# A streaming encoder layer on one core: the samples' key tiles in a pool of their own, the rope tables in a small pool, a norm factor among the constants

## The chip, the cores and the metric

The kernel runs on one core of a Trainium2 chip. The metric is device time in microseconds; of several runs of a kernel the median counts. The engines are TensorE (PE; its weight loads are PEld), VectorE (DVE), ScalarE (ACT), GpSimd (POOL) and SyncE (SP), which issues most of the transfers. ACT issues some transfers too.

## What is computed

One layer for 1024 tokens of a prompt and for 8 batches of 16 new tokens ("samples") with 1024 cached positions each. Cut to what matters here:

```python
u, g_pool, c_q, c_kv, k_r, g_mla = split(rms_norm(x, norm_g) @ w_in)
pool_out = multiscale_pool(...) * silu(g_pool)
q = (rms_norm(c_q, q_norm_g) @ w_uq).reshape(B, T, 8, 128 + 64)
q_nope = rms_norm(q[..., :128], q_nope_g)
q_rope = apply_rope(rms_norm(q[..., 128:], q_rope_g), cos, sin)
ckv_all = concat([ckv_hist, rms_norm(c_kv, kv_norm_g)])    # the samples' history is the cache
krope_all = concat([krope_hist, apply_rope(rms_norm(k_r, k_rope_g), cos, sin)])
kv = (ckv_all @ w_ukv).reshape(B, S, 8, 128 + 128)
k_nope, v = rms_norm(kv[..., :128], k_nope_g), kv[..., 128:]
attn = chunk_causal_attention(q_nope, q_rope, k_nope, krope_all, v)
h = x + concat([pool_out, attn * silu(g_mla)]) @ w_out
y = h + sigmoid(rms_norm(h, ple_norm_g) @ w_ple_gate + b_ple_gate) * (p @ w_ple)
```

All values are float32.

## The kernel before

Every product of float32 numbers is formed from high and low parts in three matmuls (`mm3`, lines 77 to 79); `split` (lines 68 and 69) makes the parts, the high one mostly on ACT (`ch`, `wh`, `m3h`, `qhl`), the low one on DVE (`cl`, `wl`, `m3l`). The phases are: 1, the input projection; 2, normalised latents and the prompt's keys, values and queries, a tile of 128 tokens at a time; 4, attention of the samples over their cache, then of the prompt, a head at a time, with pieces of the output projection (`f`) in between; 5, the rest of the output projection, the gate and the embedding. The per-layer embedding's projection (class `Embed`) is cut into units that are laid between other products where TensorE would wait: six matmuls into the one bank `p`, a copy `ev` on DVE (line 500; two buffers), and a store `ple<-ev` from ACT's queue (line 501); the next unit's weights `wraw<-w_ple` are loaded from ACT's queue as well (line 492).

**Phase 2.** `latent` loads a tile's raw latents (`rawcq`, `rawckv`), scales them and splits them (`cqh`, `cql`). `keys` forms keys and values (bank `pb`), evicts the values to `vv` and stores them (line 614). `queries` multiplies with the weights `wq` (four groups of two loads `raw<-w_uq`, split to `wqh`, `wql`), takes inverse norms (`inv_norms`: squares at lines 583 and 585, sums at 586, mean at 587, Newton steps at lines 86 to 90), applies them (line 595), and turns the rope part with the tables `qc` and `qs` (lines 640 and 332 to 335). `keys_out`, `queries_out` and `rotary_out` transpose (bank `pt`), evict (lines 625, 654 and 666) and store kT, qT and qrT. `queries_out` multiplies with the column `gqk`, the product of two norm gains and the scale.

**The samples' attention** (`attend_samples`). `keys(b, f)` loads half a batch's cached latents (`raw<-cache_T`, 512 KB) and rope keys (`kraw<-cache_krT`, two loads of 128 KB) and splits them to `ch`, `cl` and `ks`; `scores` forms the keys (bank `k`) for their norms and the scores; `queries(b)` splits the mapped queries of a batch into `m3h`, `m3l` and `qhl`, of which `m3h` and `m3l` also hold the last head of w_k (lines 1104 and 1105). `weigh` is the softmax and its product, in banks `aux`.

**Memory and order.** On-chip memory is handed out in pools. Those on the left side form a stack: during phase 2 these are p2a (value weights wvh and wvl, raw loads, `gqk`), p2c (latents, wq, the rope tables), p2b (all else). After phase 2 the pool p4k of the samples takes their place, at the same addresses. A tile waits for the last readers of what lay at its place (`reuse_waits="tile"`). The order of instructions on each engine isn't written by hand: a scheduler goes through the program with a timeline of its own and takes each engine's next instruction. It takes a new pool only when the pools whose place it uses have been given up, so a pool's place decides when the first instructions that use its tiles can be ordered. Transfers go round eight lanes; an issue waits for the transfer before it on its lane.

Of the kernel before, what the change touches and what calls it, by code (L numbers as in the profile page):

```python
# [6 lines left out]
F32R = mybir.dt.float32r  # L7
# [5 lines left out]
DRAM = bass.MemoryType.DRAM  # L13
# [6 lines left out]
P = 128  # L20
KT = D // P
TB = 384
# [16 lines left out]
class K:  # L39
    """Shared handles: the context, constants and small helpers."""  # L40
# [6 lines left out]
    def later(self, gen):  # L47
        """Start a piece of work that TensorE's next blocks of products interleave with."""
        if next(gen, self) is not self:
            self.queue.append(gen)  # L50

    def tick(self):
        """Take each piece under way to its next stop."""
# [9 lines left out]
    def split(self, hi, lo, src, scale=None, eng=None):  # L63
        """src (times a per-partition scale) as hi + lo, each of float32r's width."""
# [9 lines left out]
    def mm3(self, out, sh, sl, mh, ml, start, stop):  # L74
        """out += (sh + sl)^T (mh + ml) without the product of the two low parts."""
# [5 lines left out]
    def rsqrt(self, pool, y, v, tag):  # L81
        """y = v ** -0.5 for v > 0, by Newton steps from an exponent-halving seed."""
# [10 lines left out]
    def spread(self, pool, ps, out, r):  # L93
        """out[:, j * P + q] = r[q, j] on every partition."""
# [9 lines left out]
def load_w(k, wp, src, chunks=range(KT // WKC), scales=None, bufs=5):  # L104
    """Row chunks of a column tile of a weight [128, KT, 128], as hi and lo tiles of WKC row tiles."""
# [17 lines left out]
def project(k, ps, w, xh, xl, kts=range(KT)):  # L123
    """psum[128, TB] = w^T x over the row tiles kts, of which x holds just these."""
# [6 lines left out]
def phase1(k, sc):  # L131
    """Input projection, gates, pooling mixer, rope key; low-rank latents and row factors to DRAM.

    Stops once where the next phase's first loads can start.
    """
    tc, nc, io = k.tc, k.nc, k.io
    es, left = ExitStack(), ExitStack()
    # the first block's input leaves before the others'
# [14 lines left out]
    # order of the column tiles: latents and rope key first, gates of B last  # L153
# [19 lines left out]
    # x^T times the norm's gain, split; the row factors of the first norm  # L173
    w0 = {}
    with tc.tile_pool(name="p1x", bufs=1, side="right", reuse_waits="tile") as xp:
        for t in range(NT):
            # the very first pieces are short
# [13 lines left out]
    def row_factor(xp, t, j):  # L191
        """Sums of squares of token tile j of block t; after the last one the block's row factors, in steps."""
# [14 lines left out]
    def latent_factor(lp, kind, t, acc):  # L207
        """The row factors of a block's latents, from the lanes' sums of squares."""
# [28 lines left out]
    # latents: raw projections and their row factors, normalised where they are read back  # L237
# [41 lines left out]
    # gates and the pooling mixer; a group's map follows one block behind its input  # L279
# [37 lines left out]
def rope_tables(k, pool, tcos, tsin, gain2, scale):  # L317
    """Cosine and signed sine tables of all positions times the gain of the element they meet."""
# [1062 lines left out]
```

## Time and profile before

| | |
|---|---|
| Runs | 2322.14, 2326.36, 2325.97 us; median 2325.97 |
| Span of the profiled execution, from its first to its last instruction | 2321.7 us |
| The profiled execution's own time, with what lies around the span | the profile gives none |
| Busy PE, DVE, ACT, POOL | 2263.2, 1153.4, 844.8, 382.3 us |
| Mean granted clock of TensorE | 0.990 |
| Moved by DMA | 271.05 MB |

"Busy" counts the time in which an engine's instructions run; matmuls are pipelined, so a busy PE isn't at its peak. The granted clock is the share of TensorE's full speed: in this profile it is 1.0 or 0.5 in any short stretch, and 0.990 over the span means that some stretches ran at 0.5. A row of waits reads: the engine and line that waited, for what, us in total, times, the longest. A row of the timeline reads: start, length, engine, line, operation, output from input, count, and in brackets the idle time before it and what ended it. SPq and ACTq are the queues in which SP and ACT issue transfers; the length there is that of the issue, not of the transfer.

### The profile page before, as it was taken

The page shows a single profiled execution, that of the slowest core. Times are in us where ns is not written, and L with a number is a line of the kernel's source. Part 1 is how long each engine was busy: PE and PEld are TensorE (multiplying, and loading weights), DVE is VectorE, ACT ScalarE, POOL GpSimd, SP SyncE. Part 2 cuts the span into 40 slices and gives each one's busy share as a digit, 9 for nine tenths or more (in the row PEclk, how much of TensorE's full clock was granted, in tenths as well). Part 3 has the DMA queues.
Part 4 walks back from the last instruction along what each step waited for, and adds up shares of the span by engine and source line. Part 5 has one row for each costly group of instructions (what it writes and reads, how often), then busy time and mean ns, then how long its engine had stood idle before and what let it go on. Part 6 is the DMA issues. An engine that isn't in the chain of part 4 may idle for free.

```text
span 2321.7 us, 35417 instructions
## 1 busy us (share of the span) xinstructions
PE 2263.2 (97%) x13198; PEld 2207.8 (95%) x13198; DVE 1153.4 (50%) x2636; ACT 844.8 (36%) x1967; POOL 382.3 (16%) x357
## 2 busy tenths in 40 slices
PE   8899999999999999989999799999999999999999
PEld 8899999999999989978898699999999999999998
DVE  6443111334312169868988865555553335344343
ACT  6421111111111166766665453434342234222222
POOL 0000000123300000014443342212002221111110
PEclk9999999999999999999999899999999999999999
DMA  7522212333312186573221663434263334223221
GB/s 279 171 98 69 74 65 82 70 88 92 81 61 75 47 244 185 152 221 104 83 68 54 217 204 126 152 128 150 88 190 100 110 106 130 85 86 101 85 86 63
DMA packets 219661, 271.05 MB, mean 117 GB/s; under 512 B 38112, under 2 KB 160480, under 8 KB 219488
## 3 DMA queue, kind: packets, MB, share of 16 engines
q1 hardware_dynamic: 199616, 242.43, 33.4%
q10 hardware_dynamic: 19872, 26.35, 3.4%
q8 instruction: 104, 1.70, 0.3%
q14 instruction: 69, 0.57, 0.1%
HBM read 196.10 MB, written 72.61 MB: 116 GB/s over the span
## 4 chain that ended last, share of the span: by engine, by line
PE 80%; DVE 8%; DMA 7%; issue 2%; ACT 1%; POOL 1%; SPq 0%; ACTq 0%; DVEq 0%; POOLq 0%
PE mm L79 18%; PE mm L77 18%; PE mm L78 18%; PE f L77 3%; PE f L79 3%; PE f L78 3%; DMA xnat<-xN 2%; PE k L78 2%; PE k L77 2%; PE k L79 2%; PE t L919 1%; PE pb L77 1%; PE pb L79 1%; PE o L79 1%; PE pb L78 1%
## 5 line engine op out<-in xcount | busy, mean ns | idle before, releaser
L77 PE MATMUL mm<-A0h,wh 128*128 128x384 f32 x736 | 250.3, 340 | 6.7 <-ACT A0h L71 5.9
L78 PE MATMUL mm<-A0h,wl 128*128 128x384 f32 x736 | 249.7, 339 | 1.0 <-DVE wl L69 1.0
L79 PE MATMUL mm<-A0l,wh 128*128 128x384 f32 x736 | 249.8, 339 | 0.0
L77 PE MATMUL mm<-A1h,wh 128*128 128x384 f32 x736 | 246.6, 335 | 0.2 <-ACT ev L263 0.2
L79 PE MATMUL mm<-A2l,wh 128*128 128x384 f32 x736 | 246.6, 335 | 0.0
L77 PE MATMUL mm<-A2h,wh 128*128 128x384 f32 x736 | 246.5, 335 | 0.0
L78 PE MATMUL mm<-A2h,wl 128*128 128x384 f32 x736 | 246.4, 335 | 0.0
L79 PE MATMUL mm<-A1l,wh 128*128 128x384 f32 x736 | 246.3, 335 | 0.1
L78 PE MATMUL mm<-A1h,wl 128*128 128x384 f32 x736 | 246.3, 335 | 0.0
L69 DVE TENSOR_TENSOR wl<-wraw,wh 128x512 fp32r<-128x512 f32 (+1 forms) x232 | 157.4, 679 | 153.4 <-ACT wh L68 147.7
L68 ACT ACTIVATE wh<-wraw 128x512 fp32r<-128x512 f32 (+1 forms) x236 | 137.4, 584 | 246.8 <-PE mm L79 193.6
L77 PEld LDWEIGHTS mm<-A0h,wh 128*128 128x128 f32 x736 | 139.3, 189 | 7.4 <-ACT A0h L71 5.9
L78 PEld LDWEIGHTS mm<-A0h,wl 128*128 128x128 f32 x736 | 139.2, 189 | 1.8 <-DVE wl L69 1.8
L79 PEld LDWEIGHTS mm<-A0l,wh 128*128 128x128 f32 x736 | 139.1, 189 | 0.2 <-DVE A0l L72 0.2
L79 PEld LDWEIGHTS mm<-A1l,wh 128*128 128x128 f32 x736 | 138.2, 188 | 1.0 <-DVE A1l L72 0.7
L77 PEld LDWEIGHTS mm<-A1h,wh 128*128 128x128 f32 x736 | 138.2, 188 | 0.8 <-ACT ev L263 0.5
L77 PEld LDWEIGHTS mm<-A2h,wh 128*128 128x128 f32 x736 | 138.2, 188 | 0.0
L79 PEld LDWEIGHTS mm<-A2l,wh 128*128 128x128 f32 x736 | 138.2, 188 | 0.0
L78 PEld LDWEIGHTS mm<-A2h,wl 128*128 128x128 f32 x736 | 138.2, 188 | 0.0
L78 PEld LDWEIGHTS mm<-A1h,wl 128*128 128x128 f32 x736 | 138.2, 188 | 0.0
L233 DVE TENSOR_TENSOR ev<-mm,R 128x384 f32<-128x384 f32 x48 | 26.8, 558 | 224.3 <-PE mm L79 224.3
L1239 DVE TENSOR_TENSOR ev<-mm,R 128x384 f32<-128x384 f32 x48 | 26.8, 557 | 174.1 <-PE mm L79 170.2
(437 smaller groups left out, 5511.6 us busy)
## 6 DMA issues: line engine op xcount, KB each, us to landing
wraw<-w_in SPq DMA_DIRECT2D x120, 256.0 KB, 3.1
wraw<-w_out SPq DMA_DIRECT2D x64, 256.0 KB, 3.6
wraw<-w_ple_gate SPq DMA_DIRECT2D x64, 256.0 KB, 3.3
xnat<-xN ACTq DMA_DIRECT2D x36, 256.0 KB, 3.5
ple<-ev ACTq DMA_DIRECT2D x48, 192.0 KB, 2.5
fev<-xT SPq DMA_DIRECT2D x48, 192.0 KB, 2.4
hp<-fev SPq DMA_DIRECT2D x48, 192.0 KB, 1.9
ev<-hp SPq DMA_DIRECT2D x48, 192.0 KB, 2.3
```

The source lines that it names most:

```text
L68: nc.scalar.activation(hi, src, AF.Copy)
L69: eng.tensor_tensor(lo, src, hi, ALU.subtract)
L77: mm(out, sh, mh, start=start, stop=False)
L78: mm(out, sl, mh, start=False, stop=False)
L79: self.last = mm(out, sh, ml, start=False, stop=stop)
L233: nc.vector.tensor_tensor(ev[:], ps[:, :TB], R[t][:], ALU.mult)
L919: nc.tensor.transpose(tp[:, x, :], e[:, (c + x) * P:(c + x + 1) * P], k.ident[:])
L1239: nc.vector.tensor_tensor(g[:], ps[:, :TB], R[t][:], ALU.mult)
```

## The change

The column `gqk` moves from p2a to the pool of the constants. The rope tables and their gain come to a new small pool p2d, between p2c and p2b. `raw`, `ch`, `cl`, `kraw` and `ks` of the samples come to a new pool p4c just beneath p4k; both are closed together. The addresses of all tiles stay within 32 bytes of what they were (those of the key tiles: from the place of wvh to that of the first wq groups); the instructions and their number are the same. Comments and docstrings are gone too, with their lines kept, so that line numbers rise by 1 from 741 on and by 2 from 997 on.

```diff
-    gqk = k.t(pl, [P, 1], "gqk")
+    gqk = k.t(k.cp, [P, 1], "gqk")
...
     pq = es.enter_context(tc.tile_pool(name="p2c", bufs=1, reuse_waits="tile"))
+    pr = es.enter_context(tc.tile_pool(name="p2d", bufs=1, reuse_waits="tile"))
     pw = es.enter_context(tc.tile_pool(name="p2b", bufs=1, reuse_waits="tile"))
...
-    qc = k.t(pq, [P, 9, DR], "qc")
-    qs = k.t(pq, [P, 9, DR], "qs")
-    rope_tables(k, pq, qc, qs, io["q_rope_g2"], SCALE)
+    qc = k.t(pr, [P, 9, DR], "qc")
+    qs = k.t(pr, [P, 9, DR], "qs")
+    rope_tables(k, pr, qc, qs, io["q_rope_g2"], SCALE)
...
-    kp = tc.tile_pool(name="p4k", bufs=1, reuse_waits="tile")
-    kb = kp.__enter__()
+    kp = ExitStack()
+    kc = kp.enter_context(tc.tile_pool(name="p4c", bufs=1, reuse_waits="tile"))
+    kb = kp.enter_context(tc.tile_pool(name="p4k", bufs=1, reuse_waits="tile"))
...
-        raw = k.t(kb, [P, 2, HK * P], "raw", bufs=2)
+        raw = k.t(kc, [P, 2, HK * P], "raw", bufs=2)
...
-        ch = k.t(kb, [P, 2, HK * P], "ch", F32R, bufs=3)
-        cl = k.t(kb, [P, 2, HK * P], "cl", F32R, bufs=3)
+        ch = k.t(kc, [P, 2, HK * P], "ch", F32R, bufs=3)
+        cl = k.t(kc, [P, 2, HK * P], "cl", F32R, bufs=3)
...
-        kraw = k.t(kb, [P, HK * P], "kraw", bufs=2)
+        kraw = k.t(kc, [P, HK * P], "kraw", bufs=2)
...
-        ks = k.t(kb, [P, HK * P], "ks", F32R, bufs=2)
+        ks = k.t(kc, [P, HK * P], "ks", F32R, bufs=2)
...
-    kp.__exit__(None, None, None)
+    kp.close()
```

What it moves shows in the order of each engine. The first place is the passage from phase 2 to the samples. SP before: the stores of kT, qrT and qT of the last tiles, then the cache's first loads (the number in a name is that of its buffer).

```order
L656 DMA qT_96<-T_9309 128x8x128
L626 DMA kT_94<-T_9323 128x8x128
L668 DMA qrT_97<-rT_9568 128x4x128
L656 DMA qT_96<-T_9576 128x8x128
L1016 DMA raw_9611<-cache_T 128x2x512
L1022 DMA kraw_9617<-cache_krT 64x512 x2
L1016 DMA raw_9771<-cache_T 128x2x512
L1022 DMA kraw_9777<-cache_krT 64x512 x2
```

SP now:

```order
L656 DMA qT_96<-T_9312 128x8x128
L1018 DMA raw_9618<-cache_T 128x2x512
L1024 DMA kraw_9624<-cache_krT 64x512 x2
L1018 DMA raw_9778<-cache_T 128x2x512
L1024 DMA kraw_9784<-cache_krT 64x512
L626 DMA kT_94<-T_9326 128x8x128
L668 DMA qrT_97<-rT_9571 128x4x128
L1024 DMA kraw_9784<-cache_krT 64x512
L1018 DMA raw_10046<-cache_T 128x2x512
L1024 DMA kraw_10052<-cache_krT 64x512 x2
```

The first loads of the cache have moved ahead of the last kT store and the last two qrT and qT stores; the last qT and qrT stores now stand behind eight further cache loads.

DVE at the same place, before: the mean, seed and Newton steps of query tile 7 (`v_1476`, `r_1477`, `rsa_9410`) with an `ev` and two `wl` of the embedding's units among them.

```order
L587 TENSOR_SCALAR v_1476_9394<-v_1476_9394 128x8
L666 COPY rT_9568<-pt_9569 128x512
L69 TENSOR_TENSOR wl_9907<-wraw_9904,wh_9906 128x256
L86 TENSOR_SCALAR r_1477_9395<-v_1476_9394 128x16
L88 TENSOR_TENSOR rsa_9410<-r_1477_9395 128x16
L500 COPY ev_9565<-p_9558 128x384
L89 SCALAR_TENSOR_TENSOR rsa_9410<-rsa_9410,v_1476_9394 128x16
L90 SCALAR_TENSOR_TENSOR r_1477_9395<-rsa_9410,r_1477_9395 128x16
L69 TENSOR_TENSOR wl_9923<-wraw_9920,wh_9922 128x256
L88 TENSOR_TENSOR rsa_9410<-r_1477_9395 128x16
```

DVE now, around the same steps:

```order
L500 COPY ev_9568<-p_9561 128x384
L587 TENSOR_SCALAR v_1476_9397<-v_1476_9397 128x8
L69 TENSOR_TENSOR cl_9621<-raw_9618,ch_9620 128x1024
L1027 TENSOR_TENSOR ks_9627<-kraw_9624,ks_9627 64x512
L86 TENSOR_SCALAR r_1477_9398<-v_1476_9397 128x16
L69 TENSOR_TENSOR wl_9930<-wraw_9927,wh_9929 128x256
L500 COPY ev_9924<-p_9917 128x384
L88 TENSOR_TENSOR rsa_9413<-r_1477_9398 128x16
L69 TENSOR_TENSOR wl_9946<-wraw_9943,wh_9945 128x256
```

`cl` and `ks` of the first key tile stand between the mean (line 587) and the seed (line 86); before, they stood behind the last rT copy. A second `ks` stands further on among the Newton steps.

Ahead of that on DVE now, right after the last key tile's norms:

```order
L595 TENSOR_TENSOR kn_9244<-kn_9244,r_1460_9280 128x512 x2
L1106 COPY m3h_1540_9631<-wkh_6960 128x2x128
L1107 COPY m3l_1541_9632<-wkl_6961 128x2x128
L1106 COPY m3h_1542_9633<-wkh_6960 128x2x128
L1107 COPY m3l_1543_9634<-wkl_6961 128x2x128
L500 COPY ev_9536<-p_9529 128x384
L69 TENSOR_TENSOR m3l_1541_9632<-qp_7121,m3h_1540_9631 128x2x128
L69 TENSOR_TENSOR qhl_9653<-qr_7122,qhl_9653 128x128
L69 TENSOR_TENSOR m3l_1543_9634<-qp_7121,m3h_1542_9633 128x2x128
L69 TENSOR_TENSOR qhl_10042<-qr_7122,qhl_10042 128x128
L587 TENSOR_SCALAR v_1476_9397<-v_1476_9397 128x8
```

The four copies and the low parts of `m3` and `qhl` stood behind line 335, the end of query tile 7's rotation, before. ACT's four high parts moved likewise: they now stand between the last eviction of query tile 7 (line 636) and its last two squares, and the first `ch` stands behind the second `wh` after them, ahead of a load `wraw<-w_ple` and a store `ple<-ev`.

The second place is the start of phase 2. SP before:

```order
L692 DMA mask_8572<-own 128x8
L235 DMA gm_12_71<-ev_7109 128x384
L547 DMA rawcq_7143<-cq_6_65 128x4x128
L547 DMA rawckv_1048_7195<-ckv_3_62 128x2x128
L321 DMA ropeg_7208<-q_rope_g 128x128
L322 DMA qc_7206<-rope_cos 128x576
L323 DMA qs_7207<-rope_sin 128x576
L548 DMA srow_7456<-s_cq_28_87 128x128
L538 DMA raw_7171<-w_uq 128x768
L555 DMA ckvT<-rawckv_1048_7195 256x1x128
L538 DMA raw_7175<-w_uq 128x768
L614 DMA v_95<-vv_7215 128x8x128
```

SP now:

```order
L321 DMA ropeg_7211<-q_rope_g 128x128
L322 DMA qc_7209<-rope_cos 128x576
L323 DMA qs_7210<-rope_sin 128x576
L235 DMA gm_12_71<-ev_7109 128x384
L692 DMA mask_8575<-own 128x8
L547 DMA rawcq_7146<-cq_6_65 128x4x128
L547 DMA rawckv_1048_7198<-ckv_3_62 128x2x128
L548 DMA srow_7459<-s_cq_28_87 128x128
L555 DMA ckvT<-rawckv_1048_7198 256x1x128
L614 DMA v_95<-vv_7218 128x8x128
L538 DMA raw_7174<-w_uq 128x768
L548 DMA srow_7564<-s_cq_28_87 128x128
```

The rope tables (`ropeg`, `qc`, `qs`) have moved ahead of the mask, a store of gates and the first raw latents; the first store of values has moved ahead of the two w_uq loads of group 1, which are `raw_7171` and `raw_7175` before and `raw_7174` and `raw_7178` now. They stood ahead of the store of values; now they begin right behind it. PE has more of the embedding's units ahead of the products that need these weights.

The third place is the start of the prompt's attention, where the first head's transposes and products `o` come earlier on PE, and the pieces `f` of the output projection later; DVE's `M0l`, `M1l` and `M2l` splits, which feed those, come later as well. Between the first key tiles and the last batch of the samples the order is nearly the same, as it is behind the prompt's first heads.

## The prediction

> **What bounds the kernel now.** I read the page's engine lines and its 40 slices first, to see what the time consists of.
>
> ```profile
> span 2321.7 us, 35417 instructions
> PE 2263.2 (97%) x13198; PEld 2207.8 (95%) x13198; DVE 1153.4 (50%) x2636; ACT 844.8 (36%) x1967; POOL 382.3 (16%) x357
> PE   8899999999999999989999799999999999999999
> ```
>
> TensorE (PE) is busy for 97% of the span, and the change neither adds nor removes a product. So only two things can move the time: PE's waits, and stretches at half clock. Outside the span's first slices, the slices below 9 stand near 840, 1015 and 1275 to 1330 us. I then asked for the stretches around them (columns: length; busy us and count of PE, PEld, DVE, ACT, POOL; granted clock; share of the DMA engines; GB/s).
>
> ```profile
> 835.00:850.00 15.00, 11.58 (x44) 9.85 (x43) 11.98 (x33) 8.95 (x26) 0.00 (x0) 0.73 1.01 303
> 842.05:852.29 10.24, 8.39 (x27) 7.88 (x26) 5.35 (x18) 4.74 (x10) 0.00 (x0) 0.50 1.02 323
> 850.00:1005.00 155.00, 154.44 (x895) 144.94 (x894) 129.45 (x410) 112.45 (x399) 2.28 (x8) 0.99 0.56 165
> 1005.00:1030.00 25.00, 17.91 (x90) 14.76 (x89) 17.85 (x48) 11.21 (x29) 0.73 (x1) 0.93 0.83 249
> 1022.96:1026.37 3.41, 1.62 (x8) 0.91 (x6) 1.26 (x3) 1.64 (x3) 0.00 (x0) 1.00 1.06 313
> 1026.37:1029.78 3.41, 2.96 (x8) 2.66 (x9) 1.98 (x4) 1.42 (x3) 0.51 (x1) 0.50 1.09 329
> 1090.00:1280.00 190.00, 179.39 (x1093) 168.61 (x1092) 169.84 (x332) 113.63 (x221) 86.22 (x52) 1.00 0.22 73
> 1280.00:1360.00 80.00, 66.18 (x342) 57.62 (x341) 66.68 (x132) 43.95 (x100) 39.76 (x33) 0.87 0.74 232
> ```
>
> Three places have something to lose or win: A, the start of phase 2 (835 to 850, 3.4 us of idle PE and a clock of 0.73); B, the passage to the samples (1005 to 1030, 7.1 us idle); D, the passage to the prompt's attention (1280 to 1360, 13.8 us idle, clock 0.87). Between them PE is full (155 us from 850) or, from 1090 to 1280 (C), held by chains whose order the change leaves alone; after 1360 the slices are all 9. The waits of PE at A and B, and one of D:
>
> ```profile
> PE pb L77 <- ACT vv L613: 1.8, 1, 1.8
> PE pb L78 <- DVE cql L69: 1.5, 1, 1.5
> ...
> PE k L77 <- ACT ch L68: 1.7, 1, 1.7
> PE k L78 <- DVE cl L69: 0.6, 1, 0.6
> ...
> PE s L77 <- ACT e L904: 1.4, 1, 1.4
> PE f L77 <- DVE fev L822: 0.9, 1, 0.9
> PE f L79 <- POOL M0l L69: 0.8, 1, 0.8
> ```
>
> **The change at B.** A pool is taken only when what lies beneath it is done with. The key tiles no longer lie over the rope tables or `gqk`, which query tile 7 reads last; so the first cache load, which SP (the engine that issues these transfers) sent at 1017.88 right behind the last qT store, now stands behind the store before that.
>
> ```profile
> 1003.61 0.36 SPq L656 DMA_DIRECT2D qT<-T  x1
> ...
> 1017.43 0.36 SPq L656 DMA_DIRECT2D qT<-T  x1
> 1017.88 0.67 SPq L1016 DMA_DIRECT2D raw<-cache_T  x1
> ```
>
> It can leave 0.45 us after that store, as now, at 1004.1, 13.8 us earlier; the rope keys' load still waits for the query weights' last reader. With the 6.5 us that such loads took (a row below) it lands at 1010.6. Gone with that are PE's waits for ch and cl, 1.7 + 0.6, and, if PE is then fuller, the stretch at half clock: 2.96 us of busy PE at 0.50 cost 1.5. Together −3.8.
>
> What is added is worked out on VectorE (DVE) and ScalarE (ACT), which feed the p units (a piece of the embedding's projection, six products, then a copy `ev`, then a store) that fill PE here, one after the other through one bank.
>
> ```profile
> 1007.24 0.56 DVE L500 COPY ev<-p 128x384 f32<-128x384 f32 x1 [4.13 <-PE p L79]
> 1010.70 0.17 DVE L86 TENSOR_SCALAR r<-v 128x16 int32<-128x16 int32 x1
> 1011.19 0.56 DVE L500 COPY ev<-p 128x384 f32<-128x384 f32 x1
> 1019.68 0.29 DVE L1104 CAST m3h<-wkh 128x256 fp32r<-128x256 f32 x1
> 1019.89 0.29 DVE L1105 CAST m3l<-wkl 128x256 fp32r<-128x256 f32 x1
> ...
> 1020.83 0.42 DVE L69 TENSOR_TENSOR m3l<-qp,m3h 128x256 fp32r<-128x256 f32 x1
> ...
> 1021.90 0.55 DVE L500 COPY ev<-p 128x384 f32<-128x384 f32 x1
> ...
> 1025.54 1.23 DVE L69 TENSOR_TENSOR cl<-raw,ch 128x1024 fp32r<-128x1024 f32 x1 [2.15 <-ACT ch L68]
> 1027.26 0.69 DVE L1025 TENSOR_TENSOR ks<-kraw,ks 64x512 fp32r<-64x512 f32 x1
> ...
> 1018.76 0.40 ACT L68 ACTIVATE m3h<-qp 128x256 fp32r<-128x256 f32 x1
> ...
> 1006.20:1008.00 1.80, 1.80 (x15) 1.76 (x14) 0.76 (x3) 1.77 (x7) 0.00 (x0) 1.00 0.08 21
> ...
> ple<-ev ACTq DMA_DIRECT2D x5, 192.0 KB, 2.0
> ...
> raw<-cache_T SPq DMA_DIRECT2D x3, 512.0 KB, 6.5
> ...
> ple<-ev ACTq DMA_DIRECT2D x4, 192.0 KB, 5.0
> ```
>
> On DVE, cl and two ks come into the middle of query 7's normalisation: 1.23 + 2 × 0.69 = 2.6. Out of it go the four m3 copies, 0.2 from start to start, so 0.8, which now fall into the idle 4.13, and the four m3l and qhl splits (1020.83 to 1021.90, 1.1), which move in front. Net +0.7. ACT's four splits of the same tiles now stand ahead of query 7's squares, but two p units lie between those and the step that needs them (L86, 1010.70), so I cost that at nothing; without this cover it is at most 4 × 0.40 = 1.6.
>
> The dearer item is in the rows of `ple<-ev`, the store of an ev: median 2.0 us to landing from 1006 to 1017.3, 5.0 from there to 1032, with cache loads under way. ev has two buffers, so an ev waits for the store of two units before. Two units took 1011.19 − 1007.24 = 4.0; with 5.0 of store and 0.56 of copy it is 5.6, so +1.6 for each two units that run beside cache loads. The first six loads are 1.5 MB (2 × 512 and 4 × 128 KB), 4.9 us at the 313 GB/s of the row from 1022.96; more follow when ch is split. That is one to two pairs out of four, +1.6 to +3.2; I take 2.2, nearer the low end, because the DMA engines are at a share of 0.08 just before 1008. B: −3.8 + 0.7 + 2.2 = −0.9. Ends: −3.8 if all of it hides, and, with two pairs, ACT's 1.6 and the half clock kept, −2.3 + 0.7 + 3.2 + 1.6 = +3.2.
>
> The Trainium skill (TensorE: Matmul & The Clock Gate, "HAM oscillation — how this bites in real kernels") says that PE falls to half clock after idle gaps over about 3.4 us. The rows differ: the half-clock stretch from 1026.37 follows one with PE busy 1.62 of 3.41 us, and no wait at B is over 1.7. By that rule the 1.5 of clock would not hang on these waits, and the whole sum would be −0.9 in place of −2.4; by the rows it goes when the stretch before is more than half busy.
>
> **The change at A.** The rope tables' loads move ahead of the first latents', and the first v store ahead of the w_uq loads of group 1.
>
> ```profile
> 828.63 0.33 SPq L235 DMA_DIRECT2D gm<-ev  x1
> 831.32 0.53 SPq L547 DMA_DIRECT2D rawcq<-cq  x1
> ...
> 836.71 0.58 ACT L613 ACTIVATE vv<-pb 128x512 f32<-128x512 f32 x1
> ...
> 839.43 5.96 DMA v<-vv
> 845.47 0.61 ACT vv L613
> ```
>
> The last two rows are of the chain of waits: the v store took 5.96, vv's buffer waited for it, and PE for vv, 1.8. vv was complete at 837.3 (836.71 + 0.58), so the store can leave about 1 us earlier, at 838.4, and without two loads of 384 KB before it (2.4 us at 323 GB/s): landing 842 to 844.4 instead of 845.39, so the wait of 1.8 shrinks by 1 to 1.8; I take 1.4. The half-clock stretch (8.39 busy at 0.50, 4.2 lost) spans three equal parts of 3.41; a shorter wait may spare none or one of them (1.4), and I take 0.4. rawcq goes behind 640 KB of tables (2 × 288 and 64 KB), 2.0 us at 323 GB/s; but SP stood still for 2.3 us before it (828.96 to 831.32), and three issues of 0.3 to 0.5 fit in there: +0.3. The two w_uq loads go 1.6 us later (512 KB); the order puts p units in front of the products that need them, so nothing, and 1.6 if that cover is gone. A: −1.4 − 0.4 + 0.3 = −1.5. Ends: −7.5 (both waits, 3.3, and all 4.2), and +3.6 (2.0 + 1.6).
>
> **At D** pieces of the output projection (f) come later among the first head's scores, and transposes and o products earlier. The three waits quoted are 3.1; f being later favours M0l and fev, while softmax chains with fewer f products beside them speak against it. I take 0, with −3.1 and +3.1 as ends. C: 0, same order.
>
> **Sum**: −0.9 − 1.5 + 0 = −2.4 against the profiled span of 2321.7, so 2319.3. The profile gives no time around the span; the three runs stand 0.4 to 4.7 above it. Against their median, 2325.97, I forecast 2323.6.
>
> **Rivals.**
> 1. Slower, at B. ch stands in ACT's queue ahead of two p units' loads and stores, and cl in DVE's ahead of L86. ACT gets to ch between the second and the third ev of before, about 1010 to 1011 (an estimate from the rows at 1007.24 and 1011.19); if the cache load lands later than that (with 6.5 us it comes at 1010.6), everything behind waits one for one, and all four pairs of units run beside loads, 4 × 1.6 = 6.4, and the half clock stays: −2.3 + 0.7 + 6.4 = +4.8. It decides from 1 us of lateness on. With A at 0: 2330.8. Against it: the share of 0.08 just before. The Trainium skill (DMA: Bandwidth & Descriptors, "Issuing engines are not separate DMA queues") has transfers of all queues interleave on the same 16 engines, so that ACT's stores would pay for SP's loads; the store rows at B agree, 2.0 against 5.0.
> 2. Faster, beyond what runs can miss: A's half clock goes with its waits (−6 of the −7.5) and B stays at −0.9: 2325.97 − 6.9 = 2319.1. For it: 842.05 follows right on the two waits. Against: the first wait (cql) has no reason to go.
> 3. Nothing follows: the loads come earlier and PE meets the same total of waits, since the p units run through one bank at DVE's pace: 2326.
> 4. D loses its 3.1, and A 1.6 by the w_uq loads, while B stays: −0.9 + 3.1 + 1.6 = +3.8, so 2329.8; 0.9 more, by f products that M0l keeps waiting, and it counts as slower.
>
> **Numbers.** Three runs of one kernel spread over 4.2 us, so 0.2% (4.65 us) is about what can be told from no change. My case and rival 3, between −4.6 and +4.6: 0.34 + 0.18 = 0.52. Rival 2, with kindred gains at D: 0.28. Rival 1: 0.13; rival 4: 0.07. Faster 0.28, same 0.52, slower 0.20. The range leaves out a tenth at each side: down to 2316 (A −7.5 with D at −2.5), up to 2331.5 (rival 1 with a little more).
>
> **What would show it.** Right: first raw<-cache_T issued before 1006; no wait of k for ch or cl; the v store issued ahead of w_uq group 1 and the wait for vv under 1 us; idle PE from 1005 to 1030 between 5 and 8 us. Wrong: ple stores over 5 us from 1008 on and p waiting 2 us and more for ev; cql later than 842; over 15 us of idle PE or more than 10 us of lost clock from 1280 to 1360; a changed clock where no order changed.

## The result and the profile after

The changed kernel takes 2340.20 us (median of 4 runs, 2337.62 to 2342.86) where the kernel before took 2326.16 beside it (4 runs, 2322.14 to 2329.96): a ratio of 1.0061, with a 95% interval of 1.0046 to 1.0075. It is slower, by 14.0 us; 2323.6 was forecast, and the range ended at 2331.5.

The head of the profile after, with the busy times and PE's slices:

```profile
span 2335.8 us, 35429 instructions
PE 2270.1 (97%) x13198; PEld 2212.1 (95%) x13198; DVE 1160.7 (50%) x2636; ACT 844.2 (36%) x1967; POOL 382.4 (16%) x357
PE   8899999999999989989999799999999999999999
```

The execution's own time is 2337.62, so 1.8 us lie around the span. The products are the same 13198, but PE is busy 6.9 us longer; the 12 more instructions are waits for semaphores. To find where the span's 14.1 us came in I took, from each trace, the starts of the first product of phase 2 (keys and values), of the samples' first product k and of the first score s of the prompt's attention, and the ends of phase 2's last product and of the last score. These cut the span into six stages (us). Where the expectations below speak of phase 5 at 607 or 612 us, they count from the last score to the last product; the column "output" goes on to the span's end, 5.4 to 5.7 us later.

| Kernel | phase 1 | phase 2 (has A) | passage (B) | samples (C) | prompt's attention (has D) | output | span |
|---|---|---|---|---|---|---|---|
| before | 826.9 | 179.2 | 19.4 | 300.7 | 383.0 | 612.4 | 2321.7 |
| after | 823.3 | 187.0 | 23.2 | 298.4 | 386.1 | 617.8 | 2335.8 |
| after − before | −3.6 | +7.8 | +3.8 | −2.3 | +3.1 | +5.4 | +14.1 |

So the stages of A, B and D each got longer, where −1.5, −0.9 and 0 were forecast. The forecast for B reaches further than the passage, though: its window ran to 1032, and before the passage ends at 1025.56, so that the stretch at half clock (1026.37 to 1029.78) and the wait of k for cl lie in the samples' stage there. Passage and samples together got 1.5 us longer. And two stages moved in which no engine's order differs (but for the place of `gqk`'s own instruction), phase 1 and the output.

**A, the start of phase 2.** The same stretch of 46.7 us of before and of after (columns as in the prediction's stretches); phase 2 begins at its start in after, and 3.6 us into it before:

```profile
823.30:870.00 46.70, 43.06 (x209) 39.10 (x208) 31.23 (x78) 31.41 (x97) 0.00 (x0) 0.89 0.81 245
```

```profile
823.30:870.00 46.70, 38.38 (x183) 32.56 (x182) 31.32 (x80) 29.22 (x91) 0.00 (x0) 0.96 0.81 248
```

Counted over 46.7 us from each kernel's own first product of phase 2, it is 210 products before and 182 after. The clock is better than before, 0.96 against 0.89, yet PE did 28 products fewer. The chain of waits of after at this place says what came late, and the table of PE's waits from 820 to 870 who paid:

```profile
825.88 6.25 DMA qc<-rope_cos
832.13 0.02 issue
832.15 3.96 DMA rawcq<-cq
836.11 0.02 issue
836.14 0.42 DVE rawcq L550 x2
```

```profile
PE p L78 <- DVE wl L69: 2.5, 2, 1.3
PE p L79 <- DVE l L69: 2.0, 1, 2.0
PE p L77 <- ACT h L68: 1.1, 1, 1.1
PE p L77 <- DVE ev L500: 1.0, 2, 0.7
PE p L77 <- DVE r L90: 0.7, 1, 0.7
```

The wait for vv is gone, as forecast. But SP sent rawcq only when the cosine table had landed, 6.25 us after the table's own issue. Before, SP had stood ahead of rawcq too; the table of its waits has this row for rawcq's line:

```profile
SPq L547 <- DMA raw<-w_uq: 2.3, 1, 2.3
```

In both kernels rawcq's issue waits for the transfer that went before it on its lane. Before, that is a load of w_uq; in the new order it is the cosine table, and the mask's load, one issue ahead, waits 3.5 us for the rope gain's in the same way. The first query product starts 14.8 us after the first product of phase 2 (11.5 before), and the embedding's p units, which the order now has stand in for it, are not fed in time. A smaller part of the 7.8 comes later in phase 2: PE waits 1.6 us for an ev up to 918.6, and a stretch at half clock follows (919.7 to 923.1) that before doesn't have.

**B, the passage.** PE's waits of after from 1000 to 1040, and the half-clock stretch in it (7.62 us busy at 0.50 in 10.2 us, and a second one of 3.4 from 1032.3; before, one of 3.4):

```profile
PE p L77 <- DVE ev L500: 3.0, 1, 3.0
PE pt L665 <- DVE qr L335: 2.1, 1, 2.1
PE p L77 <- DVE v L587: 1.1, 1, 1.1
PE p L77 <- DVE rsa L89: 0.7, 1, 0.7
```

```profile
1018.70:1028.90 10.20, 7.62 (x25) 6.71 (x26) 8.80 (x19) 4.43 (x8) 5.04 (x2) 0.50 0.96 307
```

k waits for ch and cl no more, and the first cache load left at 1007.75, 0.45 us behind the qT store at 1007.30, as forecast. Instead PE waits four times on DVE, in query tile 7's chain. What held DVE shows in its rows and POOL's:

```profile
1019.08 2.35 POOL L69 TENSOR_TENSOR cl<-raw,ch 128x1024 fp32r<-128x1024 f32 x1 [109.97 <-DMA qrT<-rT]
1026.20 2.69 POOL L69 TENSOR_TENSOR cl<-raw,ch 128x1024 fp32r<-128x1024 f32 x1 [4.77 <-DMA wraw<-w_ple]
```

```profile
1016.07 1.22 DVE L69 TENSOR_TENSOR cl<-raw,ch 128x1024 fp32r<-128x1024 f32 x1
1017.32 0.69 DVE L1027 TENSOR_TENSOR ks<-kraw,ks 64x512 fp32r<-64x512 f32 x1
...
1019.83 0.56 DVE L500 COPY ev<-p 128x384 f32<-128x384 f32 x1 [1.29 <-DMA ple<-ev]
1020.31 1.15 DVE L88 TENSOR_TENSOR rsa<-r 128x16 f32<-128x16 f32 x1
...
1022.12 0.17 DVE L88 TENSOR_TENSOR rsa<-r 128x16 f32<-128x16 f32 x1
...
1024.23 0.43 DVE L69 TENSOR_TENSOR wl<-wraw,wh 128x256 fp32r<-128x256 f32 x1
...
1027.13 2.05 DVE L69 TENSOR_TENSOR wl<-wraw,wh 128x256 fp32r<-128x256 f32 x1
```

Three things. cl and ks stand in the chain, 1.9 us, as forecast. The copy ev waited 1.29 for the store of an earlier ev: the stores sent from 1011 to 1024 took 3.7 to 5.4 us to land, where those from 1009 to 1018 before took 2.0 to 3.4. And two instructions are stretched: an rsa of 1.15 us where the next takes 0.17, a wl of 2.05 where another takes 0.43. Both end as POOL's low parts of the second and third half batch end (1021.46 beside 1021.43; 1029.18 beside 1028.89), which before started only at 1029. The Trainium skill has a rule for this (SBUF — State Buffer, "SBUF: two separate sides"): VectorE and GpSimd share one pair of memory ports under an exclusive lock; an operation of VectorE with two inputs in SBUF, the on-chip memory in which the tiles lie, needs it against a GpSimd operation that reads SBUF, and whichever comes second stands until the other is done. The rows agree: rsa and wl read two tiles and stood, while ev, which reads a bank, took its usual 0.56 inside POOL's 2.35. So do the whole traces of before and after: of `wl<-wraw,wh` and of ks, all 14 and all 9 that began well inside a POOL operation of over 1 us took over one and a half times their usual time, and of the copies ev and pv out of a bank none of 3 and none of 12. The trace of before had one just behind the stretch that the prediction read: a ks of 1.58 us at 1030.64 in place of 0.69, beside POOL's split of 1029.27.

How much all of it cost shows at the end of query tile 7's rotation (line 335), before and then after:

```profile
1019.09 0.68 DVE L335 TENSOR_TENSOR qr<-qr,qtmp 128x512 f32<-128x512 f32 x1
```

```profile
1030.61 0.69 DVE L335 TENSOR_TENSOR qr<-qr,qtmp 128x512 f32<-128x512 f32 x1
```

From the end of phase 2's products to there it is 13.6 us before and 21.0 after; from there to the first product k, 5.8 and 2.2. So 3.6 us were gained behind the rotation, and the chain ahead of it lost 7.3.

**D.** At the first head of the prompt's attention after waits longest here, first PE, then ACT:

```profile
PE o L77 <- ACT pth L921: 4.2, 3, 2.8
```

```profile
1365.10 0.52 ACT L68 ACTIVATE M2h<-mraw 128x384 fp32r<-128x384 f32 x1 [1.56 <-DMA mraw<-mixp]
1367.02 0.63 ACT L870 ACTIVATE stk<-raw 128x512 fp32r<-128x512 f32 x1 [1.39 <-DMA raw<-qrT]
1367.55 0.37 ACT L921 ACTIVATE pth<-t 128x256 fp32r<-128x256 f32 x1
```

pth stands in ACT's queue behind a split that waits 1.56 us for its load, and one that waits 1.39 for another.

**Phase 1 and the output.** Two stretches of full clock, 600 us of phase 1 and 160 of the output, of before and then of after:

```profile
200.00:800.00 600.00, 600.00 (x3452) 599.89 (x3451) 157.25 (x303) 96.73 (x167) 66.18 (x104) 1.00 0.25 74
1740.00:1900.00 160.00, 160.00 (x925) 160.00 (x925) 53.58 (x92) 47.31 (x92) 39.09 (x39) 1.00 0.33 105
```

```profile
200.00:800.00 600.00, 600.00 (x3465) 599.89 (x3464) 157.42 (x298) 97.69 (x168) 66.06 (x104) 1.00 0.27 74
1740.00:1900.00 160.00, 160.00 (x908) 160.00 (x907) 53.54 (x90) 47.11 (x90) 38.40 (x39) 1.00 0.35 108
```

PE never idles in either, and the clock is 1.00; but 925 products of the same size became 908: 173.0 ns each became 176.2. In phase 1 it went the other way.

So the theories for the runs were: the rope pool's order costs A; the early cache loads cost B (and with it D); the constants' 32 bytes change the pace of the products. The rivals: the chance of single runs, p4c, and within B the late stores, the early splits on DVE, or POOL's lock.

### The profile page after: what moved, and what is told of

Same layout as the page of the kernel before. It is cut to its first block, busy times and chain, and to the rows that moved or that the text cites. A ratio compares the mean times of both kernels' runs of the same rounds, so it can differ in the third digit from the quotient of the medians.

```text
span 2335.8 us, 35429 instructions
## 1 busy us (share of the span) xinstructions
PE 2270.1 (97%) x13198; PEld 2212.1 (95%) x13198; DVE 1160.7 (50%) x2636; ACT 844.2 (36%) x1967; POOL 382.4 (16%) x357
## 4 chain that ended last, share of the span: by engine, by line
PE 82%; DMA 7%; DVE 7%; ACT 2%; issue 2%; POOL 1%; SPq 0%; ACTq 0%; DVEq 0%; POOLq 0%
PE mm L77 18%; PE mm L78 18%; PE mm L79 18%; PE f L77 3%; PE f L79 3%; PE f L78 3%; DMA xnat<-xN 2%; PE k L79 2%; PE k L77 2%; PE k L78 2%; PE t L920 1%; PE pb L77 1%; PE pb L78 1%; PE pb L79 1%; PE s L77 1%
```

## The experiments

Each ran with the kernel before beside it on the same chip, whose medians were 2326.64 (first four), 2326.55 (next four), 2326.33 (e9, e10) and 2325.43 (e11, e12). Ratios are to those, with 95% intervals.

**The parts alone.** e1: only `gqk` among the constants, the order of products unchanged:

```diff
-    gqk = k.t(pl, [P, 1], "gqk")
+    gqk = k.t(k.cp, [P, 1], "gqk")
```

> Only the norm factor gqk among the constants; every engine's order is that of before but for gqk's own instruction, and all later addresses lie 32 bytes higher. Order theory (the loss is in the new order at the start of phase 2, at the passage to the samples and in the prompt's attention): same as before, within 3 us; phase 5, from the last scores to the last product, 607 us as before. Address theory (the 32 bytes slow TensorE's stream in phase 5, which took 5.7 us longer after the change, and speed it in phase 1): 2 to 6 us slower, phase 5 near 612 us.

Measured: 2328.26 (11 runs), ratio 1.0008 (0.9999 to 1.0017). The stages of its profile: phase 1 825.7, output 617.9 (before 612.4), the rest within 1 us. In the same two stretches its counts are those of after:

```profile
200.00:800.00 600.00, 600.00 (x3465) 599.89 (x3464) 158.08 (x310) 97.17 (x167) 66.05 (x104) 1.00 0.27 74
1740.00:1900.00 160.00, 160.00 (x907) 160.00 (x906) 52.33 (x88) 46.09 (x89) 38.04 (x38) 1.00 0.34 102
```

So the pace comes with the column's move alone; as a whole it is worth +1.6 us and can't be told from nothing by the time. From the last score to the last product it is 612.2 us, as the address theory had it.

e2: only the rope tables in their small pool:

```diff
+    pr = es.enter_context(tc.tile_pool(name="p2d", bufs=1, reuse_waits="tile"))
...
-    rope_tables(k, pq, qc, qs, io["q_rope_g2"], SCALE)
+    rope_tables(k, pr, qc, qs, io["q_rope_g2"], SCALE)
```

> Only the small pool for the rope tables. Phase 2 stands in the order of the changed kernel, the caches' loads stay behind the last qT store. Order theory: the 7.8 us that phase 2 lost, from its first product to its last, are all there; the 3.8 us of the passage to the samples are not; some 8 to 11 us slower than before, 2334 to 2337. Rival (the early cache loads are what costs): within 4 us of before. Address theory: nothing in phase 5, since no address moves by 32 bytes.

Measured: 2335.10 (5 runs), 1.0032 (1.0019 to 1.0044). Phase 2 takes 187.9 us (before 179.2), as in after; the passage 18.9, since without the column's move the cache loads stay behind the last qT store; phase 1 and the output 826.9 and 611.2, as before. The prompt's attention takes 389.1, 6 more. So this one pool costs A without any early cache load, and in this profile D loses without one too.

e3: both together, and no p4c:

> The whole change without the samples' pool p4c: every engine's order is that of the changed kernel. If p4c does nothing, 2340 us as the changed kernel, 14 slower than before; if its place matters for waits at run time, up to 4 us different at the passage to the samples.

Measured: 2338.44 (5 runs), 1.0046 (1.0033 to 1.0058). Every engine's order is that of after, and so are the stages: 823.3, 188.0, 24.6, 297.8, 385.5, 619.3. The key tiles' own pool, the part that the change is named for, does nothing that these runs can tell; it is the column and the rope tables that let the cache loads go early.

e4: the kernel before once more, with a word of a comment changed:

> The kernel before once more, for the spread of the profile: if phases 1 and 5 differ between executions of one kernel by 3 us or more, their differences after the change (phase 1 3.6 us shorter, phase 5 5.7 us longer) are no doing of the change; if they repeat within 1 us, something in the change moves them. Time within 2 us of before.

Measured: 2326.53 (11 runs), 0.9993 (0.9984 to 1.0002). The stages of its profile are 826.3, 180.4, 20.3, 302.2, 384.8 and 612.2: up to 1.8 us from those of the first profile, and 4.7 in the span. Of single profiles, then, a difference of 1 or 2 us in a stage says nothing. Phase 1 and the output repeated within 0.6.

**The pace of the products.** e5: after's order, with the column as wide as 64 bytes, so that the pools behind it move by 64 in place of 32:

```diff
-    gqk = k.t(pl, [P, 1], "gqk")
+    gqk = k.t(k.cp, [P, 16], "gqk")[:, :1]
```

(and the rope pool as above)

> gqk with 64 bytes a partition instead of 4 (which take 32), and the rope pool: every engine's order is that of the changed kernel, but addresses above the constants move by 64 bytes in place of 32. Address theory: phase 1 and phase 5 as before (phase 5 607 us instead of 612), so 2.3 us less than the 2338.4 to 2340.2 of the changed order: 2336 to 2338. If the 32 bytes are not the cause, 2338.4 to 2340.2 and phase 5 at 612.

Measured: 2340.97 (5 runs), 1.0061 (1.0049 to 1.0074). A miss: the output stays slow (617.1), so it isn't the place modulo 64 that counts.

e7: the kernel before with 32 unused bytes ahead of phase 1's left tiles alone, in a pool that is closed long before the output:

```diff
+    k.t(ap[0], [P, 8], "pad")
```

> The kernel before, with 32 unused bytes at the bottom of phase 1's left pool and nowhere else; the order is that of before. It moves the one third of phase 1's moving operands (A0h, A0l) that lay at a multiple of 64 bytes to 32 beyond one. Address theory: phase 1's stream 174.4 to 173.5 ns a product, 3.2 us less: 2323.4, faster than both kernels. Otherwise as before, 2326.6.

Measured: 2324.05 (11 runs), 0.9985 (0.9977 to 0.9994). This is the fastest of all kernels here: phase 1's better pace without the output's worse one.

```profile
200.00:800.00 600.00, 600.00 (x3466) 599.89 (x3465) 158.17 (x305) 97.18 (x167) 66.04 (x104) 1.00 0.27 74
1740.00:1900.00 160.00, 160.00 (x925) 160.00 (x924) 53.07 (x90) 46.93 (x91) 39.62 (x39) 1.00 0.35 106
```

e8: the column among the constants and 32 unused bytes on the right side too, so that both sides move:

```diff
+          tc.tile_pool(name="rpad", bufs=1, side="right") as rpad):
+        k.t(rpad, [P, 8], "pad")
```

> gqk among the constants, and 32 unused bytes on the right side too, so that weights and right-hand operands also move by 32: in phase 5 both operands of every product lie at multiples of 64 bytes; the order is that of before. If it is the moving operand's own place that counts (a multiple of 64 is slow), phase 5 gets slower still, 615 to 617 us, and phase 1 by 3 or more: 2337 to 2341. If it is the two operands lying differently to each other (one at 0, the other at 32 beyond a multiple of 64), phase 5 is at 607 again and phase 1 as before: 2326.6.

Measured: 2329.50 (11 runs), 1.0010 (1.0001 to 1.0018); phase 1 825.5, output 616.9. A miss again: the output stayed slow, and neither stage got slower still, so both theories fail. The right side grows downwards, so its tiles moved down by 32 bytes where the left ones moved up, and the distance between them changed by 64. The distances in the kernels so far suggested the rule that e9 put to the test. (Of a product's two inputs the stationary tile is the one loaded as weights, wh or wl here; the moving tile streams past it.) In e9 the same right-side pad, with the column where it was before, moves what lies on the right side: the split weights, and with them those moving tiles whose distance to the weights stays 0. A0 of phase 1, and A2 and the mixed rows (M0, M1, M2) of the output, lie on the left and stay.

> The kernel before, with 32 unused bytes at the end of the scratchpad from which the right-side pools grow, so that the split weights (the stationary tiles wh, wl) start at 448 modulo 512 bytes in place of 480; the left pools, and so A0h and A0l of phase 1 (384) and the mixed rows of phase 5 (32), stay where they were, and so does the order of every engine. Theory 1, the rate of the matmul stream goes by the distance of the moving tile's start from the stationary tile's, modulo 512: phase 1's distance goes from -96 to -64 bytes, and its products from 175.8 to 173.5 ns from start to start (its stage -2 to -3.5 us); phase 5's goes from +64 to +96, and its products from 173.3 to 176.7 ns (+5 us); the whole +2 us, about 2328.5. Theory 2, it goes by the moving tile's own address: nothing changes, phase 1 stays at 175.8 ns and phase 5 at 173.3, the whole 2326.5. Theory 3, neither (a chance of the run): both stages within 0.5 us of the kernel before without a pattern.

Measured: 2330.23 (11 runs), 1.0015 (1.0006 to 1.0024), +3.9 where +2 was expected; phase 1 823.2, output 619.6.

```profile
200.00:800.00 600.00, 600.00 (x3466) 599.88 (x3465) 156.87 (x298) 97.67 (x168) 66.06 (x104) 1.00 0.27 74
1740.00:1900.00 160.00, 160.00 (x908) 160.00 (x907) 51.98 (x88) 45.76 (x88) 37.44 (x37) 1.00 0.34 103
```

Those moving tiles didn't move, and both stages changed pace as the first theory had it. From start to start of successive products at full clock (worked out from the traces), by the distance of the moving tile's start from that of the stationary tile, modulo 512 bytes:

| distance | −96 | −64 | −32 and 0 | +64 | +96 | +128 |
|---|---|---|---|---|---|---|
| ns per product | 175.8 | 173.7 | 173.6 | 173.3 | 176.7 | 176.0 |
| seen in | before, phase 1 | e1, e7, e9, phase 1 | e8, e5; A1 and A2 | before, e7, output | e1, after, e9, output | e5, e8, output |

Some records are missing from the traces, and the groups are of several hundred products or more. "Output" stands for A2 and the mixed rows; A0 and A1 lie at distance 0 there and keep 173.4 to 174.2 in every kernel. The mixed rows of e6 and e10, at +128 too, have 175.5. From 64 to 96 bytes of distance a product becomes 2.1 to 3.4 ns dearer; why, the runs don't show. The dearer paces are means of a mixture: of A0's products before, over a third take 179 or 180 ns and nearly all others 173 to 176. No run tests the modulo by itself.

**A.** e6: e5 with the rope tables' loads held on SP behind the first latents; the addresses are e5's:

```diff
-        nc.sync.dma_start(raw[:], sc[nm][t][:, :, cols])
+        k.lat = nc.sync.dma_start(raw[:], sc[nm][t][:, :, cols])
...
+    with tc.issue_after(k.lat.ins):
+        rope_tables(k, pr, qc, qs, io["q_rope_g2"], SCALE)
```

> The last kernel, with the rope tables' loads held in SP's order behind the first latents' loads. The order up to query tile 7 is that of before; the early cache loads and the new order at the passage to the samples stay. If the early table loads are what cost 8 us in phase 2: phase 2 179 to 181 us again, 2328 us, 1 to 3 slower than before, by the passage to the samples (23 to 24 us instead of 19 to 20, of which the keys give 2 to 3 back). If they are not, 2336.

Measured: 2334.87 (6 runs), 1.0038 (1.0023 to 1.0053), so 6.1 us less than e5; phase 2 takes 181.1 us again (e5 190.2). In SP's timeline rawcq goes ahead of the tables, and in the same stretch PE does 212 products where after did 183 (210 from phase 2's own start, as before):

```profile
827.27 0.53 SPq L547 DMA_DIRECT2D rawcq<-cq  x1
827.85 0.62 SPq L547 DMA_DIRECT2D rawckv<-ckv  x1
828.51 0.60 SPq L321 DMA_DIRECT2D ropeg<-q_rope_g  x1
829.16 0.43 SPq L322 DMA_DIRECT2D qc<-rope_cos  x1
```

```profile
823.30:870.00 46.70, 40.99 (x212) 37.26 (x211) 31.38 (x86) 32.94 (x110) 0.00 (x0) 0.96 0.82 242
```

That is A, shown: three loads in SP's queue ahead of the latents, with the order that follows from them. For the hold brings back the order of before on every engine up to query tile 7, the place of the embedding's units too; what the late latents cost and what the units in front of them, it doesn't divide. The 2328 expected for the whole was missed by 6.9: the passage stays long (24.5), with cache loads as early as in after, and the prompt's attention takes 388.2.

**B.** e10: e6 with the first half batch's key tiles filled by POOL instead of loaded:

```diff
-        nc.sync.dma_start(raw[:], io["cache_T"][b][:, :, cols])
+        if b + f:
+            nc.sync.dma_start(raw[:], io["cache_T"][b][:, :, cols])
+        else:
+            nc.gpsimd.memset(raw[:], 1.0)
```

(and kraw likewise)

> The kernel with the norm factor among the constants (16 wide), the rope tables in their small pool and their loads held behind the first latents, and beside that the first half batch's key tiles (raw 128x2x512 and kraw) are filled by POOL with ones in place of being loaded: that part of the samples' keys is left out. Their splits (ch, cl, ks) still stand among the last query tile's work, as early as before, and the loads of the next half batch stand behind the last query store, so nothing but the 128 KB-scale traffic of those three loads is taken from the passage. Theory 1, the passage lost because the cache loads share the DMA engines with the embedding's stores and hold the embedding's copies and units of products: the stores land in 2 to 3 us again, TensorE waits under 1 us for ev between 1008 and 1036, the passage from the last key or value product to the first samples' product goes from 24.5 back to 19 to 21 us, and the whole is 4 to 6 us below the kernel with the loads (2334.9), at 2329 to 2331. Theory 2, it lost because the splits on VectorE and ScalarE stand ahead of the last query tile's chain: the passage stays at 23 us or more and the whole at 2333 to 2336.

Measured: 2337.39 (6 runs), 1.0057 (1.0044 to 1.0070), with the passage at 22.6 us: between the two theories, and its total no better than e6. The edit did not do what was expected of it: the next half batches' loads didn't stay behind the last query store but moved up, four of 512 KB between 1004.65 and 1021.45, ahead of that store at 1026.27. So one early load of five is gone, and the run can't decide between the two. It led to a third: the stores now landed in 2.2 to 2.6 us at first (5.3 again beside the next loads), and yet TensorE waited, on DVE instructions that stood beside POOL's next splits (a ks of 2.69 us in place of 0.69, an rsa of 2.38 in place of 0.17).

e11: after with POOL's later low parts held behind query tile 7:

```diff
+        if j == 7:
+            k.q7 = nc.gpsimd.tensor_copy(tmp[:, 0, :8], qr[:, 0, :8])
...
-        k.split(ch[:], cl[:], raw[:], eng=nc.gpsimd if b + f else nc.vector)
+        with tc.issue_after(k.q7.ins):
+            k.split(ch[:], cl[:], raw[:], eng=nc.gpsimd if b + f else nc.vector)
```

> The changed kernel, with GpSimd's low parts of the samples' second and later half batches (cl<-raw,ch on POOL, 2.35 and 2.69 us at 1019.1 and 1026.2 in the changed kernel) held on POOL behind a small copy of the last query tile's finished rotary queries (128x8, added). The loads stay as early as they are, and the order of SP, ScalarE, VectorE and TensorE stays the same up to the end of the last query tile. Theory 1, a long GpSimd operation holds VectorE: in the changed kernel one VectorE instruction each ended with GpSimd's (rsa<-r 1.15 us in place of 0.17, wl<-wraw 2.05 in place of 0.42, 2.6 us together), in the chain for which TensorE waits. Then both instructions take 0.2 and 0.4 us again, TensorE's waits between 1008 and 1036 fall from 7.0 us by about that, the passage from the last key or value product to the first samples' product goes from 23.2 us to 19.5 to 21, and the whole goes from 2340.2 to 2336.5 to 2338. Theory 2, the embedding's stores landing late behind the cache loads (4.4 to 5.4 us) are the cause: nothing of this changes by more than 0.7 us, the whole stays at 2339.5 to 2341.

Measured: 2337.47 (5 runs), 1.0054 (1.0042 to 1.0066); the passage 20.9 us in place of 23.2. POOL's rows, and DVE's rsa and wl at the places of the stretched ones:

```profile
1029.41 0.19 POOL L645 COPY qtmp<-qr 128x8 f32<-128x8 f32 x1 [119.28 <-DVE qr L335]
1029.70 4.93 POOL L69 TENSOR_TENSOR cl<-raw,ch 128x1024 fp32r<-128x1024 f32 x2
```

```profile
1019.33 0.17 DVE L88 TENSOR_TENSOR rsa<-r 128x16 f32<-128x16 f32 x1
...
1026.81 0.42 DVE L69 TENSOR_TENSOR wl<-wraw,wh 128x256 fp32r<-128x256 f32 x1
...
1029.73 2.64 DVE L69 TENSOR_TENSOR wl<-wraw,wh 128x256 fp32r<-128x256 f32 x1
```

The stretches left the chain, and one came back where POOL now starts, at 1029.7: a wl of 2.64 us in the first of POOL's two splits. So the lock is shown. Its price in the passage is less sure. The last Newton step of query tile 7 starts at 1024.57 in after and at 1024.32 here, where the passage begins 0.2 earlier; so the first stretch, the rsa's, cost nothing, since DVE here waits instead for two stores (0.52 and 0.97) and for a ks (0.68). From that step to the end of the rotation, where the wl stood, it is 6.7 us in after and 5.0 here:

```profile
1028.66 0.69 DVE L335 TENSOR_TENSOR qr<-qr,qtmp 128x512 f32<-128x512 f32 x1
```

That is 1.7 of the 2.3 us. And the hold did one thing more: the key tiles' buffers stay taken for longer, so that two loads of 512 KB that after sends at 1021.74 and 1028.92 leave at 1033.46 and 1036.30 here, behind the last query stores; a part by their traffic isn't excluded. Passage and samples together got only 0.6 us shorter. In the whole time it is 12.0 us above before where after had 14.0, and those two intervals overlap.

e12: the same hold put into e6:

> The same hold on POOL, in the kernel whose rope loads are held behind the first latents (2334.9 us). There GpSimd's splits ran at 1012.5 (2.59 us) and 1018.4 (2.53), and VectorE's wl<-wraw (two of them 2.93 us in place of 0.84) and qn<-qn,r (two of them 3.44 in place of 1.29) ended with them, 4.2 us over. Theory 1: the passage goes from 24.5 us to 20 to 21.5 and the whole from 2334.9 to 2330 to 2332; what then stays above the kernel before is the address effect (1.6) and the later start of the prompt's attention. Theory 2: the passage stays at 23.5 or more and the whole at 2334 to 2336. In this kernel the order of the samples' part behind the passage differs, so up to 1.5 us either way may come from there.

Measured: 2337.37 (6 runs, 2331.87 to 2340.28), 1.0047 (1.0035 to 1.0059). The passage fell from 24.5 to 20.4 us, as expected, and passage and samples together by 2.8; the whole didn't, which was a miss. In the profiled execution, the longest of the six, phase 1 took 828.5 us and the prompt's attention 391.2 (e6 822.5 and 388.2). Phase 1's order is the same in both, so its part is chance; the order of the samples and behind them differs, so D's part may be real. What holding saves at B doesn't reach the end of this kernel.

## Why the prediction was wrong

- **A, the term +0.3.** The failed step is "SP stood still for 2.3 us before it (828.96 to 831.32), and three issues of 0.3 to 0.5 fit in there". It took the 2.3 us for spare time of SP, and they were a wait of rawcq's own issue for its lane. Behind the tables that lane is the cosine table's, and rawcq stood until the table had landed, 6.25 us after the table's issue. Late latents meant late products, and the units put in front of them as cover were not fed in time either. Measured: +7.8 in after's phase 2 (185.5 to 190.2 us in the kernels with this order, 179.2 to 182.3 in the others), and 6.1 us in the whole between e5 and e6. The end of +3.6 was too low.
- **A, vv and clock.** Right in kind: the wait for vv is gone and the clock stands at 0.96 in place of 0.89; both drowned in the rest.
- **B, loads and waits.** Right: the first load 0.45 us behind its qT store, no wait of k for ch and cl. Against the forecast of −0.9 stand +1.5 in after for passage and samples together, and +2.3 to +3.2 in e3, e5 and e6; with the order of before it was −0.9 to +2.4 (e1, e4, e7, e8, e9), so the loss is small but the gain didn't come. The step that failed is "what is added", +2.9: up to the end of query tile 7's rotation it was 7.3 us. It counted cl and ks on DVE (+0.7) and the stores (+2.2), but not the splits on POOL that early loads set off; these held DVE's chain for 1.7 us of it (after against e11). The other 5.6 the runs don't divide between DVE's own splits, the late stores and the later loads. The forecast that half clock would end there also failed: the stretch grew from 3.4 to 10.2 us. Rival 1 had the sign, and two of its marks came true, stores over 5 us and a wait of p for ev of 3.0. The first load was not late for ch, but the second and third ch waited 1.6 and 1.8 us for theirs. Its +4.8 was more than passage and samples lost.
- **C, 0.** The samples took 2.3 us less. Before, k's wait for cl (0.6) and 3.4 us at half clock lie in this stage, after 2.2 us at half clock (up to 1035.7); that explains about 1 us. Of the rest no run shows the cause, and two profiles of before differ by 1.5.
- **D, 0 with ends of ±3.1.** After's stage is 3.1 longer than that of the first profile, but 383.0 to 385.0 were seen with the order of before (e1, e4, e7, e8, e9), so only 1 to 3 us are to be explained. With the new order it took 385.5 in e3 and e11 and 388.2 to 391.2 in e2, e5, e6, e10 and e12, beyond the end. Rival 4 named M0l and fev; after's trace shows pth instead, in ACT's queue behind splits that wait for loads. No run isolates D, and this is argued from the trace alone.
- **The address.** The text on the change said that tiles stay within 32 bytes of their places, and the sum gave that no price. After's profile shows +5.4 in the output and −3.6 in phase 1. The paces give about +6.5 for the 1920 products of A2 and the mixed rows in the output, and −3.1 for the 1472 of A0 in phase 1, whose stage ran from 822.5 to 828.5 in kernels of the same pace. By e1's medians it is +1.6 as a whole. "A changed clock where no order changed" was named as what would make the forecast wrong; what changed was the pace at full clock.
- **The pool of the key tiles** was taken to let the loads go. No effect of it can be told (e3).

By medians, as differences to the kernel before: e1 +1.6; from there to e6, which adds early cache loads, +6.7 (B, D and a little C); from e6 to e5, the rope loads at A, +6.1. Together 14.4, where after measured 14.0. The parts don't simply add, though: by the other path the rope pool alone is +8.5 (e2), and the column adds 3.3 to that (e3, +11.8). By the intervals each of these steps is uncertain by 2 to 5 us.

## What to carry to other kernels

When tiles become free earlier, follow all that this starts, on every queue and engine: a load that now leaves first can hold a later issue of its queue until it has landed, and the work that the load sets off can land on an engine whose ports another engine's critical chain needs. A gap in a queue is not spare time before it is known what the next issue waits for. A change that makes a transfer early is worth no more than the waits it removes, and here those of k for ch and cl were 2.3 us. And before time is put down to a new order, compare the count of products in a stretch where no order changed.

## What the runs showed of the hardware

- TensorE's pace at full clock went by where its two tiles lay to each other: 173.3 to 173.7 ns per 128x384 product at distances of −64 to +64 bytes modulo 512, 175.5 to 176.7 at −96, +96 and +128. An unused 32 bytes in the right place gained 2.5 us of 2326.6 (e7).
- A DVE instruction of 0.17 us on two tiles took up to 2.38 us while a POOL subtraction of 2.4 us ran (e10), and ended with it; copies out of a bank were not held (after).
